# Gate columns of a decoder layer in an opening stage of their own, by seven products of quarters

## Chip, core and metric

The kernel is one layer of a hybrid decoder and runs on one core of a Trainium2 chip. The metric is the time of one execution on the device in microseconds, as the median of repeated runs. The engines are TensorE (PE, with its weight loads PEld), VectorE (DVE), ScalarE (ACT), GpSimd (POOL) and SyncE (SP, whose queue issues most loads; ScalarE's own queue, ACTq, issues most stores).

## Reference, cut to what matters

All tensors are float32: 1024 tokens, model width 1024.

```
z = x @ w_in                        # 1024 x 6152 columns: u | x_lru | g_lru | q | k | v | fg | gate_logits (3 x 1024)
y_s5  = s5(u)                       # diagonal state space, gelu, weight GLU             -> 512
y_lru = gelu(g_lru) * rglru(x_lru)  # conv4, two gates, linear scan over the tokens      -> 512
y_fox = attention(q, k, v, cumsum(log_sigmoid(fg + b_f)))  # 8 heads x 64, causal, 128-query blocks -> 512
proj  = [y_s5, y_lru, y_fox] @ w_branch                    # three products 512 -> 1024
gates = sigmoid(gate_logits + b_gate)                      # one gate per branch and column
mixed = (gates * proj).sum(over branches) @ w_out
x = LN(ALPHA * x + mixed)
x = LN(ALPHA * x + (silu(x @ w_gate) * (x @ w_up)) @ w_down)   # hidden 2816
```

The gate logits are half of the columns of the first product, and only the sum of the three gated projections reads them.

## The kernel before, in words

**Arithmetic.** Each operand of a matmul is split into a rounded high part (ScalarE copies it to fp32r) and a low rest (DVE subtracts), in `split` (L142); `mm3` (L119) makes three matmuls of 128x128 by 128x512 of each product: high by high, high by low, low by high.

**Columns.** `load_x` (L179) loads 128 tokens, PE transposes them (L190) and the parts go to the tiles `x` and `m`. `zblock` (L200) makes 128 columns of z for all tokens: `wcols` (L170) loads 512 KB of weights into a staging tile `ws` (three buffers) and splits it into `wh` and `wl` (two buffers each), and `zpart` (L194) makes each half of the tokens from 8 x 3 = 24 matmuls into a PSUM tile `b` (three buffers) and hands it to a sink. The sink of a gate block (L487) takes tanh (L490) and stores the result to DRAM (`gate_d`).

**Three streams.** `fox` (L381) makes V, Q and K of a pair of heads, after those of pair 0 the forget sums, then `attention` (L360) goes through 8 heads in turn. A step of it is 128 queries: scores on PE into the single score tile `s` (L113, two PSUM banks, one buffer), a masked reduce with the head's bias row on DVE (L320 for the diagonal block with `ndk`, L323 for the columns left of it with `nck`), exp on ScalarE (L324), a scale; after two steps transposes and the value products follow. The bias row of a head comes by a broadcast load (L302) of `ck_d`, and GpSimd masks it (L303); `nck` and `ndk` have one buffer each. `others` makes the columns of u, x_lru and g_lru, then the 24 gate blocks, then the merges of branches 0 (S5) and 1 (RG-LRU): `merge` (L515) multiplies a branch by `w_branch` and by the gates that it loads again. `side` makes the S5 branch in four quarters, its GLU, and then the recurrence, whose four blocks each end with tanh, reciprocal (L848), sqrt (L850), scan (L854), a store (L857) and, for merge 1, a reload and split (`reload`, L499).

**Order.** A loop at the end takes the next step from the stream with the least accumulated cost; each `yield` adds an assumed cost, T_Z = 15 after a column block, T_AT0 and T_AT1 for an attention step. That is the program order; a scheduler with a model of the engines then sets the order of each engine's own instructions, within the data's dependences. Behind the streams come merge 2, the output product, a layer norm, and the feed-forward stage from about 1005 us on, which already works by seven products: its 22 blocks of gate and up columns use sums of quarters, with weight sums by GpSimd and evictions by DVE.

Of the kernel before, what the change touches and what calls it, by code (L numbers as in the profile page):

```python
# [13 lines left out]
F32 = mybir.dt.float32  # L14
# [23 lines left out]
T_AT0 = 1.2  # L38
T_AT1 = 0.473
T_FOX = 10.0  # L40
T_Z = 15.0
T_M = 6.16
T_S5 = 1.44
T_LRU = 1.246
# [13 lines left out]
def trunk(ctx: ExitStack, tc: tile.TileContext, A: dict, out: bass.AP):  # L58
# [12 lines left out]
    pools["side"] = side_stack.enter_context(tc.tile_pool(name="side", bufs=1, side="left"))  # L71
    pools["fox"] = fox_stack.enter_context(tc.tile_pool(name="fox", bufs=1, side="right"))


    SLOTS = {
        "x": ("sb", 8), "m": ("sb", 8), "ws": ("sb", 3), "wh": ("sb", 2), "wl": ("sb", 2),
        "s": ("side", 9), "q": ("fox", 8), "pt": ("fox", 4), "tr": ("fox", 2), "nck": ("fox", 1), "ndk": ("fox", 1),
    }

    LATE = {  # L80
        "ws": ("keep", 4), "w": ("keep", 8), "x": ("keep", 9), "m8": ("mid", 4), "ln": ("mid", 2),
# [5 lines left out]
    def name(n):  # L87
        count[0] += 1
        return f"{n}{count[0]}"

    def new(tag, dt=F32, shape=(P, 1024)):
        pool, bufs = SLOTS[tag]
        return pools[pool].tile(list(shape), dt, name=name(tag), tag=tag, bufs=bufs)

    def half_tile(dt=F32):
        return pools["sb"].tile([P, 512], dt, name=name("zs"), tag="zs", bufs=3)

    def small(shape, dt=F32, name_="c"):
        return const.tile(list(shape), dt, name=name(name_))
# [28 lines left out]
    def tt(e, o, a, b, op):  # L128
        return pin(e.tensor_tensor(o, a, b, op))  # L129
# [16 lines left out]

    ident = small([P, P], name_="ident")
    make_identity(nc, ident)
    tri = scr_([P, P])
    POOL.memset(tri, 1.0)  # L150
    POOL.affine_select(tri, tri, pattern=[[1, P]], compare_op=ALU.is_ge, fill=0.0, base=0, channel_multiplier=-1)
    ones = scr_([P, P])
    POOL.memset(ones, 1.0)
# [22 lines left out]

    x_in, w_in = A["x"], A["w_in"]

    def load_x(tb):  # L179
        h, c = tb // 4, slice((tb % 4) * P, (tb % 4 + 1) * P)  # L180
        xt = new("s")
        SP.dma_start(xt, x_in[tb * P : (tb + 1) * P, :])
        for kp in range(4):
            if tb % 4 == 0:
                XH[h][kp] = new("x", F32R, (P, 2, 512))
                XL[h][kp] = new("m", F32R, (P, 2, 512))
            pa = bank([P, 2, P], "ab"[kp % 2])
# [61 lines left out]

    NF = NT * HEADS  # L250
# [130 lines left out]
    def fox():  # L381
        order = [0, 1, 2, 3]
        for p in order:
# [58 lines left out]
    first_k = done["k"]  # L442


    rows = few("nat", [124, P], 1, "side")

    def put_rows(r, ap, c=slice(0, P)):
        SP.dma_start(rows[r : r + ap.shape[0], c], ap)

    put_rows(0, A["b_gate"].rearrange("(n p) -> n p", p=P))  # L450
    put_rows(24, A["lru_conv_w"].rearrange("k (n p) -> (k n) p", p=P))
    put_rows(40, A["lru_conv_b"].rearrange("(n p) -> n p", p=P))
    put_rows(44, A["lru_b_a"].rearrange("(n a) d -> n (a d)", a=2))
    put_rows(48, A["lru_b_x"].rearrange("(n a) d -> n (a d)", a=2))
    put_rows(52, A["lru_lambda"].rearrange("(n p) -> n p", p=P))
    put_rows(56, A["s5_b_glu"].rearrange("(n p) -> n p", p=P))
    for c in (slice(0, 64), slice(64, P)):
        put_rows(60, A["s5_a_re"], c)
        put_rows(92, A["s5_a_im"], c)
    pr = bank()  # L460
    PE.transpose(pr[:, 0:124], rows, ident[0:124, 0:124])
    cols = small([P, 124], name_="cols")
    DVE.tensor_copy(cols, pr[:, 0:124])
    half = small([P, 60], name_="half")
    ts(DVE, half, cols[:, 0:60], 0.5, ALU.mult)
# [5 lines left out]
    gate_d = dram.tile([3, NK, P, S], F32, name="gate_d")  # L471

    def plain_sink(dst):
        def sink(h, ps):
# [5 lines left out]
    def u_sink(b):  # L480
        def sink(h, ps):
            st = half_tile()
            ACT.copy(st.rearrange("p (j c) -> p c j", j=8), ps.rearrange("p (c j) -> p c j", j=8))
            ACT.dma_start(u_d[b][:, :, 64 * h : 64 * h + 64], st.rearrange("p (j c) -> p j c", j=8))
        return sink

    def gate_sink(r):  # L487
        def sink(h, ps):
            st = half_tile()
            ACT.activation(st, ps, AF.Tanh, bias=half[:, r : r + 1], scale=0.5)  # L490
            ACT.dma_start(gate_d[r // NK, r % NK][:, 512 * h : 512 * h + 512], st)
        return sink


# [853 lines left out]
```

## Time and profile before

| | |
|---|---|
| median of 3 runs | 1660.53 us (1660.35 to 1661.82) |
| profiled execution, its span | 1665.8 us, 1664.1 us |
| PE busy | 1600.4 us, 96% of the span |
| PEld | 1326.4 us, 80% |
| DVE | 1010.8 us, 61% |
| ACT | 633.9 us, 38% |
| POOL | 600.7 us, 36% |
| PE's share of the chain that ended last | 77% (DVE 8%, DMA 5%) |
| mean granted TensorE clock | 0.984 |

The span runs from the first to the last instruction of the profiled execution. Busy time counts an engine's instructions without its waits. The chain that ended last is followed back from the last instruction to whatever released each step. Shares of the whole span mix stages; the rows further below are by stage.

### The profile page before, as it was taken

The page shows a single profiled execution, that of the slowest core. Times are in us where ns is not written, and L with a number is a line of the kernel's source. Part 1 is how long each engine was busy: PE and PEld are TensorE (multiplying, and loading weights), DVE is VectorE, ACT ScalarE, POOL GpSimd, SP SyncE. Part 2 cuts the span into 40 slices and gives each one's busy share as a digit, 9 for nine tenths or more (in the row PEclk, how much of TensorE's full clock was granted, in tenths as well). Part 3 has the DMA queues.
Part 4 walks back from the last instruction along what each step waited for, and adds up shares of the span by engine and source line. Part 5 has one row for each costly group of instructions (what it writes and reads, how often), then busy time and mean ns, then how long its engine had stood idle before and what let it go on. Part 6 is the DMA issues. An engine that isn't in the chain of part 4 may idle for free.

```text
span 1664.1 us, 20521 instructions
## 1 busy us (share of the span) xinstructions
PE 1600.4 (96%) x7482; PEld 1326.4 (80%) x7482; DVE 1010.8 (61%) x1602; ACT 633.9 (38%) x960; POOL 600.7 (36%) x529
## 2 busy tenths in 40 slices
PE   8989998999989999999999998999999999999997
PEld 6877887877877888888888886888888888778886
DVE  4746575633643366967758659675555555546766
ACT  4324454433543354656213224222222222244442
POOL 0111314442234011111140017599988788500004
PEclk9999999999989999999999998999999999999999
DMA  5332233333233334335654812356544445597752
GB/s 167 75 89 72 70 91 89 93 73 95 84 74 89 97 108 143 104 120 196 220 175 155 274 51 80 123 178 202 180 162 165 165 155 175 200 336 234 243 176 101
DMA packets 219968, 236.09 MB, mean 142 GB/s; under 512 B 33376, under 2 KB 162524, under 8 KB 219868
## 3 DMA queue, kind: packets, MB, share of 16 engines
q1 hardware_dynamic: 192604, 202.83, 39.1%
q10 hardware_dynamic: 27264, 31.96, 5.9%
q8 instruction: 59, 0.97, 0.2%
q14 instruction: 41, 0.34, 0.1%
HBM read 163.96 MB, written 70.78 MB: 141 GB/s over the span
## 4 chain that ended last, share of the span: by engine, by line
PE 77%; DVE 8%; DMA 5%; issue 4%; POOL 3%; ACT 2%; SPq 1%; ACTq 0%; DVEq 0%; POOLq 0%
PE p L117 34%; PE b L117 33%; PE a L117 8%; DMA nck<-ck_d 2%; PE s L117 2%; POOL s L129 1%; PE a L341 1%; DMA ws<-w_ffn_down 1%; DVE r L129 1%; DVE s L129 1%; POOL ln L129 1%; DVE wl L129 1%; DVE m L129 1%; ACT r L1235 1%; DMA row<-ln_b 1%
## 5 line engine op out<-in xcount | busy, mean ns | idle before, releaser
L117 PE MATMUL b<-x,wh 128*128 128x512 f32 x912 | 353.6, 399 | 2.3 <-ACT s L706 1.7
L117 PE MATMUL b<-x,wl 128*128 128x512 f32 x832 | 330.0, 397 | 0.0
L117 PE MATMUL b<-m,wh 128*128 128x512 f32 x784 | 310.8, 396 | 0.0
L117 PE MATMUL p<-mx,w 128*128 128x512 f32 x1056 | 250.5, 392 | 1.8 <-DVE mx L129 1.0
L117 PEld LDWEIGHTS p<-mx,w 128*128 128x128 f32 x1056 | 200.0, 190 | 44.3 <-POOL m L129 1.4
L117 PEld LDWEIGHTS b<-x,wh 128*128 128x128 f32 x912 | 173.9, 191 | 37.1 <-ACT s L706 2.0
L117 PEld LDWEIGHTS b<-x,wl 128*128 128x128 f32 x832 | 158.3, 190 | 32.4
L129 DVE TENSOR_TENSOR x<-x,p 128x512 f32<-128x512 f32 x163 | 108.4, 683 | 109.6 <-PE p L117 92.7
L117 PEld LDWEIGHTS b<-m,wh 128*128 128x128 f32 x784 | 149.9, 191 | 29.1 <-issue 0.2
L117 PE MATMUL p<-w,w 128*128 128x512 f32 x528 | 157.5, 390 | 1.2 <-DVE w L129 1.0
L129 POOL TENSOR_TENSOR s<-s,s 128x1024 f32<-128x1024 f32 (+9 forms) x76 | 77.5, 1020 | 207.4 <-ACT s L850 73.8
L129 DVE TENSOR_TENSOR w<-ws,w 128x1024 fp32r<-128x1024 f32 x88 | 115.3, 1316 | 52.7 <-ACT w L143 52.5
L143 ACT CAST w<-ws 128x1024 fp32r<-128x1024 f32 x88 | 92.1, 1050 | 110.5 <-PE p L117 72.6
L117 PE MATMUL p<-wo,w 128*128 128x512 f32 x528 | 127.3, 389 | 0.0
L129 DVE TENSOR_TENSOR wl<-ws,wh 128x1024 fp32r<-128x1024 f32 x62 | 85.3, 1376 | 65.7 <-ACT wh L143 62.4
L117 PEld LDWEIGHTS p<-w,w 128*128 128x128 f32 x528 | 98.8, 188 | 23.3 <-DVE w L129 2.9
L117 PEld LDWEIGHTS p<-wo,w 128*128 128x128 f32 x528 | 99.1, 188 | 20.6
L143 ACT CAST wh<-ws 128x1024 fp32r<-128x1024 f32 x62 | 65.1, 1050 | 125.1 <-PE b L117 94.4
L129 DVE TENSOR_TENSOR w<-m,w 128x1024 fp32r<-128x1024 f32 x44 | 67.6, 1536 | 63.5 <-ACT w L143 63.5
L129 POOL TENSOR_TENSOR ln<-x,x 128x512 f32<-128x512 f32 x44 | 75.7, 1726 | 64.0 <-ACT x L1170 52.6
L117 PE MATMUL p<-w 128*128 128x512 f32 x264 | 97.5, 390 | 1.1 <-ACT w L143 1.1
L129 POOL TENSOR_TENSOR r<-r,row 128x1024 f32<-128x1024 f32 x7 | 16.7, 2389 | 189.9 <-DVE r L129 184.7
(276 smaller groups left out, 2730.0 us busy)
## 6 DMA issues: line engine op xcount, KB each, us to landing
ws<-w_in SPq DMA_DIRECT2D x48, 512.0 KB, 4.5
ws<-w_ffn_gate SPq DMA_DIRECT2D x27, 512.0 KB, 4.5
gate_d<-zs ACTq DMA_DIRECT2D x48, 256.0 KB, 2.0
zs<-gate_d SPq DMA_DIRECT2D x48, 256.0 KB, 2.6
ws<-w_ffn_up SPq DMA_DIRECT2D x22, 512.0 KB, 4.7
x<-w_ffn_down SPq DMA_DIRECT2D x22, 512.0 KB, 5.5
hid_d<-ln SPq DMA_DIRECT2D x22, 512.0 KB, 4.2
wts_d<-x SPq DMA_DIRECT2D x22, 512.0 KB, 2.6
```

What stands on the lines that cost most here:

```text
L117: PE.matmul(o, a, b, start=first, stop=last)
L129: return pin(e.tensor_tensor(o, a, b, op))
L143: pin(ACT.copy(hi, src))
L341: PE.transpose(ta[:, j, e, :], pts[e][:, (k0 + j) * P : (k0 + j + 1) * P], ident)
L1235: pin(ACT.activation(r, r, AF.Identity, bias=nm, scale=rs))
```

## The change

A stage ahead of everything else makes all 24 gate blocks, two at a time (12 pairs of neighbouring blocks), and stores their tanh to `gate_d` as before. For a pair the tokens are cut into two halves, the inner dimension into two halves and the two blocks are the two halves of the columns, so that the product is one of 2x2 by 2x2 quarters; it is made by seven products of sums of quarters, each 4 x 3 = 12 matmuls of 128x512, where the plain form has eight such products. The sums of x (`s1` to `s4`, split into high and low) are made once, in `load_x`, when the second half of the tokens comes in; the sums of weights are four adds per pair on GpSimd; the quarters of the result are added on DVE, and tanh reads them from SBUF. The stage has memory pools of its own, which are closed behind it. V of pair 0 becomes a plain `zblock`, the gate loop leaves `others`, the small parameter rows are loaded by ACTq, and T_Z goes from 15 to 40.

```diff
-T_Z = 15.0
+T_Z = 40.0
...
+    EARLY = {
+        "x": ("sb", 8), "m": ("sb", 8), "ws": ("early", 3), "w": ("early", 8), "t": ("early", 9), "m8": ("early", 1),
+    }
...
     def load_x(tb):
...
+            if h == 0:
+                tt(POOL, rawx[j][:, e], hi.bitcast(F32), lo.bitcast(F32), ALU.add)
+            elif kp < 2:
+                tt(DVE, s3[:, e], s3[:, e], pa, ALU.subtract)
+            else:
+                e = slice(2 * kp - 4, 2 * kp - 2)
+                tt(POOL, x22[:, e], hi.bitcast(F32), lo.bitcast(F32), ALU.add)
+                tt(DVE, s1[:, e], pas[kp - 2], x22[:, e], ALU.add)
+        if h == 0:
+            return
+        tt(POOL, s2, x22, s3, ALU.subtract)
+        tt(POOL, s4, s4, s2, ALU.subtract)
+        for n, src, e in (("s2", s2, POOL), ("s3", s3, DVE), ("s1", s1, DVE), ("s4", s4, POOL)):
...
+            ACT.copy(hi, src)
+            tt(e, lo, src, hi.bitcast(F32), ALU.subtract)
...
+    EP = [(b, d) for b in range(3) for d in range(0, NK, 2)]
...
+    EPRE = 4
...
+    def early_sums(p):
+        ER[p] = [early_cols(p, e) for e in range(2)]
...
+        tt(POOL, t1, w12, w11, ALU.subtract)
+        tt(POOL, t2, w22, t1, ALU.subtract)
+        tt(POOL, t3, w22, w12, ALU.subtract)
+        tt(POOL, t4, w21, t2, ALU.subtract)
...
+    def xop(i, k):
+        if i in (1, 2, 4):
+            h, k = {1: (0, k), 2: (0, 4 + k), 4: (1, 4 + k)}[i]
+            return xh(h, k), xl(h, k)
+        return [t[:, k] for t in SX[{3: "s4", 5: "s1", 6: "s2", 7: "s3"}[i]]]
...
+    def early_product(i, p):
+        ps = bank(tag="ba"[turns[0] % 2])
+        turns[0] += 1
+        for k in range(4):
+            mm3(ps, EW[p][i][0][:, k], EW[p][i][1][:, k], *xop(i, k), k == 0, k == 3)
+        return ps
...
+    load_x(0)
+    early_parts(0, early_cols(0, 0), 1, 2)
+    for tb in range(1, 4):
+        load_x(tb)
+    early_parts(1, early_cols(1, 0), 1, 2)
...
+    for p in range(EPRE):
+        early_begin(p)
+        early_first(p)
+        if p < 2:
+            load_x(4 + 2 * p)
+            load_x(5 + 2 * p)
+            early_parts(2 + p, early_cols(2 + p, 0), 1, 2)
+        if p == 2:
+            early_sums(0)
+            early_b(0)
+        if p == 3:
+            early_c(0)
+    pinned[0] = True
+    early_sums(1)
+    early_middle(0)
+    for p in range(len(EP)):
...
+        p5 = early_product(5, p)
...
+        tt(DVE, s1, u2, early_product(7, p), ALU.add)
+        tt(DVE, u3, s1, p5, ALU.add)
+        tt(DVE, u2, u2, p5, ALU.add)
+        early_gate(p, 1, 1, u3)
...
+        tt(DVE, s1, s1, early_product(4, p), ALU.add)
+        early_gate(p, 0, 1, s1)
+        tt(DVE, u2, u2, early_product(3, p), ALU.add)
+        early_gate(p, 1, 0, u2)
+    pinned[0] = False
...
             if p == order[0]:
-                load_x(0)
-                w = wcols(w_in, C_V + p * P)
-                for tb in range(1, NT):
-                    load_x(tb)
-                for h in range(2):
-                    zpart(w, h, v_sink)
+                zblock(C_V + p * P, v_sink)
...
-        for b in (0, 1, 2):
-            for d in range(NK):
-                zblock(C_G + b * D + d * P, gate_sink(b * NK + d))
-                yield T_Z
```

`early_begin` makes product 1 of a pair, `early_first` product 2 and with it the first quarter of the result, `early_middle` product 6. `early_parts`, `early_b` and `early_c` split the weight quarters and their sums. While `pinned` is set, copies and adds of the stage keep the order of the program.

**SyncE's queue at the start.** Before, the eight x blocks (`s`, 128x1024) follow each other, with one weight block (`ws`) among them:

```order
L182 DMA s_102<-x 128x1024
L172 DMA ws_132<-w_in 128x8x128
L182 DMA s_138<-x 128x1024
L182 DMA s_160<-x 128x1024
L182 DMA s_182<-x 128x1024
L182 DMA s_204<-x 128x1024
L182 DMA s_234<-x 128x1024
L182 DMA s_256<-x 128x1024
L182 DMA s_278<-x 128x1024
L172 DMA ws_368<-w_in 128x8x128
```

In the changed kernel the x blocks are the tiles `t`:

```order
L189 DMA t_88<-x 128x1024
L294 DMA ws_123<-w_in 128x8x128
L294 DMA ws_210<-w_in 128x8x128
L294 DMA ws_361<-w_in 128x8x128
L189 DMA t_129<-x 128x1024
L294 DMA ws_478<-w_in 128x8x128
L294 DMA ws_515<-w_in 128x8x128
L294 DMA ws_517<-w_in 128x8x128
L189 DMA t_156<-x 128x1024
L294 DMA ws_566<-w_in 128x8x128
L189 DMA t_183<-x 128x1024
```

Seven weight blocks have moved ahead of the fourth x block.

**TensorE in the first head.** Before, the scores (`s` from `q`, `q`) and value products (`a` from `tr`, `q`) of a step stand between column matmuls (`b` from `x` or `m` and a weight):

```order
L117 MATMUL b_1740<-x_227,wh_1702 128x512
L117 MATMUL a_999<-tr_1001,q_100 128x256
L117 MATMUL b_1740<-m_228,wh_1702 128x512
L117 MATMUL s_985<-q_96,q_94 128x512
L117 MATMUL s_985<-q_98,q_94 128x512
L117 MATMUL s_985<-q_96,q_94 128x256
L117 MATMUL s_985<-q_98,q_94 128x256
L117 MATMUL a_999<-tr_1001,q_100 128x256 x3
```

In the changed kernel, at the second to fourth step of the same head (transposes of the exponentials are `a` from `ident`, `pt`):

```order
L122 MATMUL s_2561<-q_2017,q_2015 128x256
L122 MATMUL s_2561<-q_2019,q_2015 128x256
L529 MATMUL a_2600<-ident_77,pt_2548 128x128
L122 MATMUL s_2574<-q_2017,q_2015 128x384
L122 MATMUL s_2574<-q_2019,q_2015 128x384
L529 MATMUL a_2600<-ident_77,pt_2560 128x128 x2
L122 MATMUL s_2587<-q_2017,q_2015 128x512
L122 MATMUL s_2587<-q_2019,q_2015 128x512
L122 MATMUL a_2599<-tr_2601,q_2021 128x256
L529 MATMUL a_2710<-ident_77,pt_2573 128x128
```

The column matmuls have left this place; three scores stand with only three transposes among them.

**TensorE behind the last block of the recurrence.** Before, the last gate matmuls of the recurrence (`b` from `s`, `s`) are followed by merge 0 (`a` from `x`, the reloaded S5 branch):

```order
L117 MATMUL b_6966<-s_6945,s_6121 128x512
L117 MATMUL b_6966<-s_6946,s_6121 128x512
L117 MATMUL b_6966<-s_6945,s_6122 128x512
L117 MATMUL a_7031<-x_6978,wl_7003 128x512
L117 MATMUL a_7031<-x_6984,wh_7002 128x512
L117 MATMUL a_7031<-x_6985,wh_7002 128x512
L117 MATMUL a_7031<-x_6984,wl_7003 128x512
```

In the changed kernel they are followed by merge 1 (`b` and `a` from `s_7520`, the first reloaded block of the recurrence's result):

```order
L122 MATMUL b_7500<-s_7479,s_6777 128x512
L122 MATMUL b_7500<-s_7480,s_6777 128x512
L122 MATMUL b_7500<-s_7479,s_6778 128x512
L122 MATMUL b_7556<-s_7520,wh_7544 128x512
L122 MATMUL b_7556<-s_7521,wh_7544 128x512
L122 MATMUL a_7573<-s_7520,wh_7544 128x512
L122 MATMUL a_7573<-s_7521,wh_7544 128x512
```

Merge 0 has moved ahead of the recurrence's last block, and nothing else stands between that block and the product that reads its result.

## Rows read from the trace of the kernel before

**Rows 1.** Stages: stretch, its length, busy us (count) per engine, granted clock, DMA.

```profile
core 0: us, PE busy (x) PEld busy (x) DVE busy (x) ACT busy (x) POOL busy (x), PEclk, DMA share, GB/s
120.00:706.00 586.00, 556.72 (x2844) 467.82 (x2845) 326.00 (x684) 270.25 (x488) 160.12 (x237) 0.97 0.34 91
706.00:826.00 120.00, 119.23 (x547) 98.70 (x546) 88.25 (x77) 56.64 (x69) 15.55 (x6) 1.00 0.52 175
1045.00:1425.00 380.00, 378.95 (x1672) 313.50 (x1671) 217.29 (x227) 103.80 (x138) 310.18 (x199) 1.00 0.51 170
```

**Rows 2.** The same view, 40 us of the feed-forward stage.

```profile
1080.00:1120.00 40.00, 40.00 (x178) 33.12 (x177) 29.24 (x29) 11.51 (x15) 37.41 (x24) 1.00 0.52 172
```

**Rows 3.** Grouped lines, ScalarE, 0 to 880 us: busy, mean ns, idle before.

```profile
L143 ACT CAST wh<-ws 128x1024 fp32r<-128x1024 f32 x60 | 63.0, 1050 | 125.1 <-PE b L117 94.4 <-PE a L117 24.8 <-DVE ho L129 3.9
L490 ACT ACTIVATE zs<-b,half 128x512 f32<-128x512 f32 x48 | 33.0, 687 | 49.8 <-PE b L117 48.9 <-issue 0.4
```

**Rows 4.** Timeline, start of the span, TensorE: start, duration, instruction, wait before.

```profile
4.85 0.66 PE L190 MATMUL a<-ident,s 128*128 128x128 f32 x2 [4.85 <-DMA s<-x]
17.83 0.50 PE L117 MATMUL b<-x,wh 128*128 128x512 f32 x1 [0.22 <-DVE m L129]
```

**Rows 5.** Grouped lines, GpSimd, whole span.

```profile
L129 POOL TENSOR_TENSOR m<-ws,m 128x512 f32<-128x512 f32 x44 | 70.6, 1605 | 1.6
L129 POOL TENSOR_TENSOR x<-x,x 128x512 f32<-128x512 f32 x28 | 40.4, 1443 | 17.5 <-ACT x L992 12.5 <-DVE x L129 3.2
L129 POOL TENSOR_TENSOR mx<-x,mx 128x512 fp32r<-128x512 f32 x7 | 10.3, 1473 | 108.3 <-ACT mx L973 108.3
L129 POOL TENSOR_TENSOR s<-s,s 128x256 f32<-128x256 f32 x8 | 6.1, 766 | 0.0
```

**Rows 6.** One tile's instructions: ns min/median/max, first and last start, forms.

```profile
L320 DVE CUSTOM_DVE_ANT_0 pt<-s,ndk x64: 216/292/306, 119.8 to 706.0; 128x128 f32<-128x128 f32 x64
L117 PE MATMUL s<-q,q x192: 220/389/735, 53.4 to 704.4; 128*128 128x512 f32 x96, 128*128 128x128 f32 x32, 128*128 128x256 f32 x32, 128*128 128x384 f32 x32
```

**Rows 7.** Grouped lines, VectorE, 0 to 880 us.

```profile
L129 DVE TENSOR_TENSOR wl<-ws,wh 128x1024 fp32r<-128x1024 f32 x60 | 82.9, 1381 | 65.7 <-ACT wh L143 62.4 <-PE b L117 2.7
L323 DVE CUSTOM_DVE_ANT_0 pt<-s,nck,st 128x896 f32<-128x896 f32 x8 | 9.2, 1145 | 0.2
```

**Rows 8.** Timeline, TensorE, 425 to 490 us: value products and small products.

```profile
448.30 0.64 PE L117 MATMUL a<-tr,q 128*128 128x256 f32 x4
449.69 2.48 PE L117 MATMUL b<-s,s 128*128 128x128 f32 x20
```

**Rows 9.** The bias row's tile: mask on GpSimd, and its load from issue to landing.

```profile
L303 POOL TENSOR_SCALAR_AFFINE_SELECT ndk<-nck x8: 1091/1091/1092, 118.7 to 648.4; 128x1024 f32<-128x1024 f32 x8
...
DMA to landing us min/median/max: 9.0/9.1/10.1
```

**Rows 10.** Timeline, change from head 0 to head 1.

```profile
149.66 0.22 DVE L320 CUSTOM_DVE_ANT_0 pt<-s,ndk 128x128 f32<-128x128 f32 x1
...
152.29 0.38 SPq L302 DMA_DIRECT2D nck<-ck_d  x1
...
161.79 0.29 DVE L320 CUSTOM_DVE_ANT_0 pt<-s,ndk 128x128 f32<-128x128 f32 x1 [7.12 <-POOL ndk L303]
```

**Rows 11.** Timeline, last block of the recurrence and first of merge 1.

```profile
782.45 1.52 PE L117 MATMUL b<-s,s 128*128 128x512 f32 x6
...
814.91 1.23 DVE L129 TENSOR_TENSOR s<-ws,s 128x1024 fp32r<-128x1024 f32 x1 [3.43 <-ACT s L143]
...
826.42 0.61 PE L117 MATMUL b<-s,wh 128*128 128x512 f32 x2
```

**Rows 12.** Stages of 5 us, end of the first layer norm.

```profile
1005.00:1010.00 5.00, 1.17 (x6) 0.63 (x4) 5.00 (x4) 2.22 (x5) 5.00 (x4) 1.00 0.00 0
1010.00:1015.00 5.00, 2.17 (x8) 1.43 (x8) 4.96 (x7) 0.15 (x1) 5.00 (x4) 0.62 0.13 52
1015.00:1020.00 5.00, 4.52 (x11) 3.56 (x12) 5.00 (x6) 2.71 (x5) 3.71 (x3) 0.50 0.13 53
```

More of the change, by code (lines that the diff above doesn't have):

```diff
@@ L70, in trunk @@
     pools = {"sb": sb, "const": const}
[L71 to L76, printed above, removed]
+    early_stack = ExitStack()
+    pools["early"] = early_stack.enter_context(tc.tile_pool(name="early", bufs=1, side="left"))
+    pools["sums"] = early_stack.enter_context(tc.tile_pool(name="sums", bufs=1, side="right"))
+    EARLY = {
+        "x": ("sb", 8), "m": ("sb", 8), "ws": ("early", 3), "w": ("early", 8), "t": ("early", 9), "m8": ("early", 1),
+    }
+    MIXERS = {
+        "x": ("sb", 8), "m": ("sb", 8), "ws": ("work", 3), "wh": ("work", 2), "wl": ("work", 2),
         "s": ("side", 9), "q": ("fox", 8), "pt": ("fox", 4), "tr": ("fox", 2), "nck": ("fox", 1), "ndk": ("fox", 1),
     }
+    SLOTS = dict(EARLY)
     LATE = {
@@ L95, in half_tile @@
     def half_tile(dt=F32):
-        return pools["sb"].tile([P, 512], dt, name=name("zs"), tag="zs", bufs=3)
+        return pools["work"].tile([P, 512], dt, name=name("zs"), tag="zs", bufs=3)
     def small(shape, dt=F32, name_="c"):
@@ L148, in trunk @@
     make_identity(nc, ident)
[L149 to L153, printed above, removed]
     eps_t = small([P, 16], name_="eps")[:, 0:1]
@@ L247, in softplus_neg, with early_cols, early_parts @@
         return p
+    gate_d = dram.tile([3, NK, P, S], F32, name="gate_d")
+    EP = [(b, d) for b in range(3) for d in range(0, NK, 2)]
+    EW = [dict() for _ in EP]
+    EG = [None] * len(EP)
+    ER = {}
+    EPRE = 4
+    def early_cols(p, e):
+        b, d = EP[p]
+        c0 = C_G + b * D + (d + e) * P
+        t = new("ws", shape=(P, NK, P))
+        SP.dma_start(t, w_in[:, c0 : c0 + P].rearrange("(k p) c -> p k c", p=P))
+        return t
+    def early_parts(p, src, i, j):
+        hi, lo = [new("w", F32R, (P, NK, P)) for _ in range(2)]
+        split(src, hi, lo)
+        EW[p][i], EW[p][j] = [[t[:, c] for t in (hi, lo)] for c in (slice(0, 4), slice(4, 8))]
@@ new lines, in early_sums, with early_b @@
+    def early_sums(p):
+        ER[p] = [early_cols(p, e) for e in range(2)]
+        w11, w21, w12, w22 = [ER[p][e][:, c] for e in range(2) for c in (slice(0, 4), slice(4, 8))]
+        t = new("m8", shape=(P, 16, P))
+        t1, t2, t3, t4 = [t[:, 4 * i : 4 * i + 4] for i in range(4)]
+        tt(POOL, t1, w12, w11, ALU.subtract)
+        tt(POOL, t2, w22, t1, ALU.subtract)
+        tt(POOL, t3, w22, w12, ALU.subtract)
+        tt(POOL, t4, w21, t2, ALU.subtract)
+        ER[p].append(t)
+    def early_b(p):
+        early_parts(p, ER[p][2][:, 0:8], 5, 6)
+        v = new("t", F32R, (P, NK, P))
+        split(ER[p][1][:, 4:8], v[:, 0:4], v[:, 4:8])
+        EW[p][3] = [v[:, 0:4], v[:, 4:8]]
@@ new lines, in early_gate, with early_begin, early_first @@
+    def early_gate(p, e, h, y):
+        b, d = EP[p]
+        r = b * NK + d + e
+        pin(ACT.activation(y, y, AF.Tanh, bias=half[:, r : r + 1], scale=0.5))
+        ACT.dma_start(gate_d[b, d + e][:, 512 * h : 512 * h + 512], y)
+    def early_begin(p):
+        t = new("t", shape=(P, 2, 512))
+        EG[p] = [t[:, 0], t[:, 1]]
+        pin(ACT.copy(EG[p][0], early_product(1, p)))
+    def early_first(p):
+        s1, y = EG[p][:2]
+        tt(DVE, y, s1, early_product(2, p), ALU.add)
+        early_gate(p, 0, 0, y)
@@ new lines, in early_middle, with put_rows @@
+    def early_middle(p):
+        t = new("t", shape=(P, 2, 512))
+        EG[p] += [t[:, 0], t[:, 1]]
+        tt(DVE, t[:, 0], EG[p][0], early_product(6, p), ALU.add)
+    load_x(0)
[3 more added lines that the diff above has]
+    early_parts(1, early_cols(1, 0), 1, 2)
+    rows = few("nat", [124, P], 1, "early")
+    def put_rows(r, ap, c=slice(0, P)):
+        ACT.dma_start(rows[r : r + ap.shape[0], c], ap)
+    put_rows(0, A["b_gate"].rearrange("(n p) -> n p", p=P))
@@ new lines, in trunk @@
+    pr = bank(tag="a")
+    PE.transpose(pr[:, 0:124], rows, ident[0:124, 0:124])
+    cols = small([P, 124], name_="cols")
+    DVE.tensor_copy(cols, pr[:, 0:124])
+    half = small([P, 60], name_="half")
+    ts(DVE, half, cols[:, 0:60], 0.5, ALU.mult)
+    for p in range(EPRE):
[10 more added lines that the diff above has]
+            early_c(0)
@@ L250, in trunk @@
+    pinned[0] = False
+    early_stack.close()
+    SLOTS.clear()
+    SLOTS.update(MIXERS)
+    pools["work"] = sb_stack.enter_context(tc.tile_pool(name="work", bufs=1, side="left", reuse_waits="tile"))
+    pools["side"] = side_stack.enter_context(tc.tile_pool(name="side", bufs=1, side="left", reuse_waits="tile"))
+    pools["fox"] = fox_stack.enter_context(tc.tile_pool(name="fox", bufs=1, side="right", reuse_waits="tile"))
     NF = NT * HEADS
@@ L442, in trunk @@
     first_k = done["k"]
[L445 to L465, printed above, removed]
     u_d = dram.tile([NB, P, 8, P], F32, name="u_d")
```

59 lines of the change are left out of this document (47 added, 12 removed).

## Prediction

> **What bounds the kernel now.** I read the busy times stage by stage first, then the grouped lines of each engine, then the order of the two programs beside the trace's timeline. TensorE (PE) is busy 1600.4 of 1664.1 us, and the stages show that it bounds nearly all of them: from the first attention step to the last (120 to 706 us) PE is busy 556.7 of 586 us while VectorE (DVE) is busy 326.0, from 706 to 826 us PE is busy 119.2 of 120, and in the feed-forward stage it never stops [rows 1]. So PE time saved is time saved, as long as PE stays the engine that the others wait for. A 128x512 matmul in a full stream costs 40 us / 178 = 0.2247 us [rows 2].
>
> The gate columns are 24 blocks; their 48 halves appear as 48 tanh evictions on ScalarE [rows 3]. Each half is 24 matmuls, so 1152 matmuls, 258.9 us of PE. They need nothing but x and weights and nobody waits for them until the merges. The order puts them between the attention steps: they are the work that PE does while DVE handles a softmax. That is the second thing the change touches.
>
> **The arithmetic.** Seven quarter products of 12 matmuls for 12 pairs are 1008 matmuls, 226.5 us. Against 258.9 that is 144 matmuls fewer, 32.4 us. Everything below is what this gain meets.
>
> **The start of the new stage.** Before, the first x block reaches PE at 4.85 us and the first column matmul runs at 17.83 us, with all eight x blocks transposed [rows 4]. After, SyncE's queue has three weight blocks ahead of x block 1, three more ahead of block 2 and one ahead of block 3, and from the fourth on a weight load waits for a staging buffer that a split must free. With the trace's first landing, and a split of 1.05 us on ScalarE plus 1.38 us on DVE behind each landing [rows 3, 7], I put block 2 at about 17, block 3 at about 21 and the first product at about 24 us. Products 1 and 2 of four pairs (96 matmuls, 21.6 us) need only the first half of x. Product 6 needs s2, a sum over the second half that GpSimd makes from block 4 on, after the first pair of products (about 32 us). Per block GpSimd does two adds of 128x256 at 0.766 us, two of 128x512 at 1.443 and two splits of 128x512 at 1.473: 7.4 us, 29.5 for four, plus one set of weight sums that stands between (four adds, 1.6 us each, 6.3 us), less the last split, which product 6 doesn't need: 32 + 29.5 + 6.3 - 1.5 = 66 us [rows 5]; I take 67. Bounds: 58, if GpSimd is as fast as its best rows and never waits, and 75, if transposes wait for PSUM buffers that GpSimd holds up.
>
> From there 912 matmuls remain, 205 us at the stream's rate. Per pair DVE has four splits and seven evictions (about 10 us), GpSimd 6.4 us, PE 18.9 us; the feed-forward stage has the same mix with PE full [rows 1, 2]. The stage ends at 67 + 205 = 272 us. Before, the gate columns and the 17.8 us ahead of them cost 276.7. So of 32.4 us about 28 go in the start, and the stage gives 5.
>
> **The first attention step.** V, Q and K of pair 0 take 144 matmuls, 32.4 us, plus 1.5 for the first weight split: K ends at 306. Before, the first score stands right behind K at 53.4 us and the first reduce comes at 119.8 [rows 6]: 66 us in which DVE builds the forget sums and S5 parameters and the bias row is stored and reloaded. Between K and the second score stand 255 matmuls of 512 columns before, with small ones 58 us of PE, and 200 after, 48 us. I take 63 us for the chain (48 if PE's work covered it): first reduce at 369 us.
>
> **The attention steps.** One PSUM tile of two banks holds every score (its pool has one buffer), so score k+1 waits for the reduces of step k: PE and DVE meet 64 times. I cut the order of each engine at these 64 places and added the trace's row durations (reduces 0.29 to 1.15 us [rows 6, 7], a value matmul of 256 columns and a small one of 128 each 0.12 us [rows 8]). From the second score to the last, before: PE 518, DVE 351 (7% above the busy time in rows 1, since short instructions overlap), and the sum over the steps of the busiest engine 550 us; the trace took 585 [rows 6]. PE led in 43 of 62 steps. After: PE 333, DVE 332, sum of the busiest 434; PE leads in only 23 steps. Column and merge matmuls between the two scores are 936 instead of 1754, and the later steps of head 0 have none. The trace shows the excess of 35 us at the head changes: the bias row is loaded once the last reduce is done, and the load takes 9.1 us to land, then GpSimd masks it in 1.09 us, so a head change takes 12 us even where little is to be done [rows 9, 10]. After, four of seven changes have 6.0, 6.0, 7.8 and 7.2 us of work in that step: 12.4 less these is 22.6 us; two at a change of pairs keep the 7 to 9 us that they have before, one has enough DVE work: 38 us together. So 369 + 1 + 434 + 38 = 842 us for the last reduce.
>
> The Trainium skill (DMA: Bandwidth & Descriptors, Anatomy of one DMA) prices a DMA at about 2.0 us plus its bytes over 436 GB/s; for this 512 KB row its estimate would be 3.2 us, head changes would nearly vanish, and the sum would be some 38 us lower. The trace's 9.1 us differs and decides here.
>
> **Behind attention.** Before, 958.1 us pass from the last reduce to the end. The order has 63.3 us less PE work there (859.5 for 922.8). But the last recurrence block loses its cover. Its matmuls end at 783.97 us; tanh, reciprocal, scan, a store, a reload and a split follow, ready at 816.14: 32.2 us, and PE enters merge 1 only at 826.42, busy with gates and merge 0 all the while [rows 11]. After, its last matmul is followed at once by merge 1, of which 12 matmuls (2.7 us) can run: 29 us of PE idle. Bounds 20 (ScalarE and the queues less crowded) and 32. Ahead of it DVE has 60 us of work for PE's 57, which I price at 3. So 842 + 958.1 - 63.3 + 32 = 1769 us of span.
>
> The profiled execution has 1665.8 us for a span of 1664.1, and the median of the runs is 1660.53: +1.7 - 5.3. **Forecast 1766 us, 6.4% slower.** By differences: -32.4 (arithmetic), +28 (start), +8 (first step), +72 (attention: 139 us over PE's work instead of 67), +32 (recurrence), about +107 with rounding.
>
> **Rivals.**
> 1. *Queues run ahead and fill the steps.* If PE and DVE overlap over a whole head rather than a step, the busiest engine by head sums to 378 instead of 434; with the start at 58, the first step's chain at 48, the head changes at 23 and the tail at 22 the span is 263 + 34 + 48 + 1 + 378 + 23 + 958 - 63 + 22 = 1664, the median about 1660: no change or a little faster. For it: before, PE is nearly full. Against it: the single score tile, and before's 585 us lie above the sum by step, not below. It takes every low end at once; with half of them it is 1700 to 1720. 9%.
> 2. *Half clock.* From 1005 to 1015 us PE worked only 3.3 of 10 us, and the granted clock fell to 0.62 and then 0.50, which is 1.2 GHz, and was still there while PE worked 4.5 of the next 5 us [rows 12]. In the 39 steps that PE doesn't lead it has 113 us of work; at half speed 44 us of it stick out over the other engines: 1810. The Trainium skill (TensorE: Matmul & The Clock Gate, What's actually happening) says that the throttled clock is the default and activity lifts it, which speaks against a stage with half-idle PE. 15%.
> 3. *The early loop isn't PE's.* Its single buffer for weight sums and three staging buffers make a ring: split, sums, split, about 15 us of a pair's 18.9. At 22 us a pair 12 pairs add 37 us: 1803. The feed-forward stage speaks against it, with more buffers. 8%.
> 4. *The start is hidden* (58 instead of 67) with the rest as forecast: 1757, inside my range.
>
> **How the numbers follow.** The forecast has 65% with its own range of 1715 to 1805. The range of 1695 to 1820 takes in half of rival 1's ends and both slow rivals and leaves out about 2 in 10. A measurement here tells 0.2% (3.3 us) from no change. Faster: two thirds of rival 1, 6%; same: 3%; slower: 91%.
>
> **What would show it.** Product 6 waiting for GpSimd at 60 to 70 us; PE full from there to about 270; first reduce near 369; in attention PE waiting for reduces (L320 and L323 of before) in long total, a PE share near 70% and several stretches of low clock; head changes of 12 us; one PE gap near 29 us ahead of merge 1; the feed-forward stages unchanged. If PE is still over 90% busy from the first reduce to the last, the step argument is wrong; if the first product 6 runs before 50 us, the start is.

## Result: 1797.5 us for 1661.2, and the profile after

The changed kernel takes 1797.47 us (median of 4 runs, 1795.4 to 1799.05), the kernel before 1661.17 beside it (1660.35 to 1663.83). The ratio is 1.0817, 95% interval 1.0798 to 1.0836: slower by 136 us, where 105 were forecast. The time lies inside the stated range, at its upper part.

The page of the profiled execution after, its head:

```profile
span 1796.8 us, 20639 instructions
PE 1613.0 (90%) x7338; PEld 1327.2 (74%) x7338; DVE 1099.9 (61%) x1734; ACT 672.6 (37%) x1012; POOL 708.3 (39%) x614
...
PE   5799997879789879886776999899999999999997
...
PEclk9899998979999889997797999899999999999999
```

There are 144 matmuls less, and TensorE is busy 12.6 us longer. Busy time times one less the granted clock, summed over the span, is 51 us for 18 before: in TensorE's busy time the low clock alone takes back the 32.4 us of arithmetic. The other 12 us are not traced to a place; matmuls that stand alone, without overlap, are the likely one. Its idle time grew from 63.7 to 183.8 us. Where that lies, the stages of the changed kernel show (columns as in [rows 1]):

```profile
core 0: us, PE busy (x) PEld busy (x) DVE busy (x) ACT busy (x) POOL busy (x), PEclk, DMA share, GB/s
0.00:70.00 70.00, 40.58 (x163) 32.19 (x164) 38.65 (x68) 31.89 (x63) 53.45 (x58) 0.88 0.48 143
70.00:276.00 206.00, 206.00 (x910) 170.65 (x910) 94.35 (x121) 72.27 (x94) 51.82 (x41) 1.00 0.33 103
276.00:286.00 10.00, 1.24 (x4) 0.70 (x4) 1.29 (x2) 1.76 (x2) 0.00 (x0) 0.66 0.65 181
286.00:330.00 44.00, 42.61 (x183) 34.15 (x182) 15.81 (x32) 14.20 (x21) 0.96 (x1) 0.96 0.27 61
330.00:390.00 60.00, 45.62 (x204) 35.77 (x203) 43.31 (x175) 14.74 (x19) 18.30 (x16) 0.93 0.36 73
390.00:861.00 471.00, 396.82 (x2005) 328.31 (x2006) 296.86 (x665) 235.93 (x438) 158.55 (x234) 0.91 0.31 82
861.00:957.00 96.00, 62.39 (x273) 51.26 (x272) 77.67 (x67) 37.75 (x46) 15.86 (x6) 0.82 0.33 111
1175.00:1555.00 380.00, 378.30 (x1669) 313.07 (x1668) 220.42 (x228) 103.74 (x137) 312.35 (x200) 1.00 0.51 170
```

The first line is the start of the stage, with TensorE idle 29 of 70 us; the second its full part, with no idle time; then the hole between the stage and V, then V, Q and K, the first step's chain, attention (74 us idle at a clock of 0.91, where [rows 1] have 29 us and 0.97), the recurrence's tail (34 us idle), and the feed-forward stage, which is as it was.

The stage's first product and its first product 6 (`sx` are the sums of x), on TensorE:

```profile
23.82 0.78 PE L122 MATMUL b<-x,w 128*128 128x512 f32 x1
...
69.69 2.52 PE L122 MATMUL b<-sx,w 128*128 128x512 f32 x10
```

The hole behind it, on all engines: the stage's last gate store, V's weight load, its split, and V's first matmul.

```profile
278.17 0.33 ACTq L341 DMA_DIRECT2D gate_d<-t  x1
280.26 1.98 SPq L172 DMA_DIRECT2D ws<-w_in  x3
...
284.32 1.04 ACT L148 CAST wh<-ws 128x1024 fp32r<-128x1024 f32 x1 [6.18 <-DMA ws<-w_in]
...
285.42 0.80 PE L122 MATMUL b<-x,wh 128*128 128x512 f32 x1 [8.76 <-ACT wh L148]
```

In attention the reduce and the mask answer to [rows 6] and [rows 9]. The last two lines are the time that VectorE sat idle ahead of the 64 diagonal reduces, and how often, by what ended it: the mask or the score.

```profile
L508 DVE CUSTOM_DVE_ANT_0 pt<-s,ndk x64: 261/291/294, 389.6 to 861.4; 128x128 f32<-128x128 f32 x64
L491 POOL TENSOR_SCALAR_AFFINE_SELECT ndk<-nck x8: 1093/1093/1094, 388.5 to 809.4; 128x1024 f32<-128x1024 f32 x8
...
  POOL ndk L491: 38.4, 5
  PE s L122: 30.9, 16
```

The tail ahead of merge 1 answers to [rows 11]; first VectorE's part of the recurrence's last block, then TensorE:

```profile
933.09 6.54 DVE L996 RECIPROCAL s<-s 128x1024 f32<-128x1024 f32 x1
...
944.63 2.29 DVE L1002 TENSOR_TENSOR_SCAN s<-s,s 128x1024 f32<-128x1024 f32 x1
...
955.42 1.22 DVE L134 TENSOR_TENSOR s<-ws,s 128x1024 fp32r<-128x1024 f32 x1 [6.11 <-ACT s L148]
```

```profile
927.72 2.43 PE L122 MATMUL b<-s,s 128*128 128x512 f32 x10
956.85 1.22 PE L122 MATMUL b<-s,wh 128*128 128x512 f32 x2 [26.70 <-ACT wh L148]
```

TensorE has nothing between the recurrence's last matmuls and merge 1, and its first two matmuls of merge 1 take 1.22 us where [rows 11] have 0.61.

A table that the rest uses, from the traces (us): the first reduce, from there to the last reduce, and from there to the end.

| kernel | first reduce | attention | behind it | span |
|---|---|---|---|---|
| before | 119.8 | 586.2 | 958.1 | 1664.1 |
| changed | 389.6 | 471.8 | 935.4 | 1796.8 |
| b_nogates | 117.5 | 473.0 | 976.8 | 1567.3 |
| b_front | 382.0 | 493.8 | 939.1 | 1814.9 |
| a_h8 | 303.8 | 507.3 | 945.3 | 1756.4 |
| a_h4 | 231.4 | 550.9 | 964.2 | 1746.5 |

In one line: the gate columns now cost 269.8 us ahead of the first reduce, and their absence gives back 137.1 behind it (114.4 in attention, 22.7 later). The difference is the 132.7 us of the spans.

### The profile page after: what moved, and what is told of

Its sections match the earlier page's. It is cut to its first block, busy times and chain, and to the rows that moved or that the text cites. A ratio compares the mean times of both kernels' runs of the same rounds, so it can differ in the third digit from the quotient of the medians.

```text
span 1796.8 us, 20639 instructions
## 1 busy us (share of the span) xinstructions
PE 1613.0 (90%) x7338; PEld 1327.2 (74%) x7338; DVE 1099.9 (61%) x1734; ACT 672.6 (37%) x1012; POOL 708.3 (39%) x614
## 4 chain that ended last, share of the span: by engine, by line
PE 51%; DVE 10%; DMA 5%; ACT 3%; issue 2%; POOL 2%; SPq 0%; ACTq 0%; DVEq 0%; POOLq 0%
PE p L122 31%; PE b L122 12%; PE a L122 6%; DMA nck<-ck_d 2%; DVE s L134 1%; DMA ws<-w_ffn_down 1%; DVE s L142 1%; DVE r L134 1%; DVE pt L511 1%; PE s L122 1%; PE a L529 1%; DVE pt L138 1%; POOL ln L134 1%; DVE x L142 1%; POOL s L134 1%
## 5 line engine op out<-in xcount | busy, mean ns | idle before, releaser
L122 PE MATMUL b<-x,wh 128*128 128x512 f32 x528 | 202.7, 404 | 19.1 <-ACT wh L148 8.8
L122 PE MATMUL b<-x,wl 128*128 128x512 f32 x448 | 179.3, 400 | 0.0
L122 PE MATMUL b<-m,wh 128*128 128x512 f32 x400 | 159.9, 400 | 0.0
L134 DVE TENSOR_TENSOR w<-m,w 128x1024 fp32r<-128x1024 f32 x68 | 97.7, 1436 | 85.5 <-ACT w L148 85.4
L122 PEld LDWEIGHTS b<-x,wh 128*128 128x128 f32 x528 | 101.5, 192 | 41.8 <-ACT wh L148 9.2
L134 POOL TENSOR_TENSOR m<-ws,m 128x512 f32<-128x512 f32 x68 | 100.7, 1481 | 2.5
L134 POOL TENSOR_TENSOR m<-ws,ws 128x512 f32<-128x512 f32 x34 | 50.6, 1488 | 125.6 <-DVE w L134 108.0
L122 PEld LDWEIGHTS b<-x,wl 128*128 128x128 f32 x448 | 86.3, 193 | 18.6 <-DVE wl L134 0.8
L122 PE MATMUL a<-tr,q 128*128 128x256 f32 (+1 forms) x320 | 72.8, 322 | 24.7 <-DVE tr L134 16.8
L148 ACT CAST w<-m 128x1024 fp32r<-128x1024 f32 x68 | 71.1, 1046 | 63.4 <-PE p L122 45.5
```

The source lines that it names most:

```text
L122: PE.matmul(o, a, b, start=first, stop=last)
L148: pin(ACT.copy(hi, src))
```

## Experiments

Ratios are to the kernel before, run on the same chip at the same time.

**b_nogates: the gate columns left out of the kernel before.**

```diff
-        for b in (0, 1, 2):
-            for d in range(NK):
-                zblock(C_G + b * D + d * P, gate_sink(b * NK + d))
-                yield T_Z
+        zblock(C_G, gate_sink(0))
+        yield T_Z
...
-                SP.dma_start(g, gate_d[n, d][:, hs])
+                SP.dma_start(g, gate_d[0, 0][:, hs])
```

> The kernel before with 23 of its 24 gate blocks left out (the merges read the first block's gates in their place), so 1104 matmuls or 248 us of TensorE work less, all of it from between the attention steps. Theory 'cover': the mixers take what their steps' dependences take; the changed kernel, whose mixers have no gate columns either, spends 1796.8 - (330.1 - 53.4) = 1520 us of span outside its early stage, so about 1518 us here, 140 below the kernel before, and two thirds as much TensorE idle time in attention as in the changed kernel or more. Rival 'TensorE bounds': the time falls by the matmuls' own 248 us to about 1413.

Measured: 1568.12 us, ratio 0.9425 (0.9407 to 0.9443). Without 248 us of TensorE's work the kernel is 94 us shorter. That is far from the rival's 1413; it is also 50 us longer than my 1518. Attention is as forecast, 473.0 us beside 471.8 in the changed kernel:

```profile
118.00:590.00 472.00, 403.33 (x2021) 332.74 (x2022) 288.10 (x657) 221.24 (x427) 155.86 (x235) 0.90 0.29 78
590.00:727.00 137.00, 64.61 (x268) 51.24 (x267) 96.17 (x78) 50.06 (x59) 20.53 (x8) 0.72 0.27 92
```

The excess is behind it (976.8 us for 935.4), where with the column step at 15 three waits of the recurrence stand bare on TensorE:

```profile
663.78 1.65 PE L117 MATMUL b<-s,s 128*128 128x512 f32 x3 [15.14 <-ACT s L143]
...
690.86 1.65 PE L117 MATMUL b<-s,s 128*128 128x512 f32 x3 [19.72 <-ACT s L143]
...
726.84 1.22 PE L117 MATMUL b<-s,wh 128*128 128x512 f32 x2 [28.54 <-ACT wh L143]
```

So the gate columns were nearly two thirds hidden in the kernel before.

**b_front: the move alone, with eight products.** The loop over the gate blocks and the rows that it needs stand ahead of V; `T_Z = 40.0`:

```diff
+    load_x(0)
+    w = wcols(w_in, C_G)
+    for tb in range(1, NT):
+        load_x(tb)
...
+    for h in range(2):
+        zpart(w, h, gate_sink(0))
+    for r in range(1, 24):
+        zblock(C_G + r * P, gate_sink(r))
```

> The kernel before with its 24 gate blocks, still eight products, moved whole ahead of V, Q and K of pair 0 (no sums, no seven products; the column step 40 as in the changed kernel). Theory 'cover': the move alone makes it slow. The blocks end at 17.8 + 1152 x 0.2247 = 277 us, about where the early stage of the changed kernel ends, V follows without a wait, and the rest is as in the changed kernel: about 1780 us. Rival 'the stage itself' (its sums, its start, its ring of buffers are what costs): the move alone costs little, 1660 to 1700 us.

Measured: 1813.74 us, ratio 1.0905 (1.0883 to 1.0928). The move, with the column step that goes with it, costs 151 us; the rival, that the stage's sums and start do it, falls. It is also 34 us above my 1780, 22 of them in attention. Its first score comes at 322.6 us, TensorE being full until there, and that of the changed kernel at 330.3: up to this point the seven products give nothing, they lose 8 us, which is no more than the hole of 8.8 that b_front doesn't have. The 16 us by which the changed kernel is nevertheless faster are in attention, 471.8 for 493.8. The mixers' work is the same in both; in b_front's order VectorE does 20 us more of the side work ahead of the last reduce (317.4 us busy for 296.9), and nothing of it comes back behind it (939.1 for 935.4):

```profile
382.00:876.00 494.00, 412.56 (x2047) 339.87 (x2047) 317.40 (x675) 242.81 (x447) 165.83 (x236) 0.89 0.30 82
```

An order alone is thus worth some 20 us here, which has to be kept in mind for small differences below.

**a_ws: staging buffers in the pool that stays open.**

```diff
-        "x": ("sb", 8), "m": ("sb", 8), "ws": ("early", 3), "w": ("early", 8), "t": ("early", 9), "m8": ("early", 1),
+        "x": ("sb", 8), "m": ("sb", 8), "ws": ("sb", 3), "w": ("early", 8), "t": ("early", 9), "m8": ("early", 1),
```

(and the same for `ws` of the mixers.) 

> The changed kernel, with the weights' staging buffers kept in the pool that stays open, so that V's weight load need not wait for memory of the early stage. Theory: of the 9.0 us in which TensorE waits between the early stage and V (276.4 to 285.4 us) 7 to 9 go, 1788 us. Rival: the load waits for its place in SyncE's queue or for its buffers anyhow: within 2 us of 1797.

Measured: 1817.46 us, ratio 1.0928 (1.0906 to 1.0949). V's weights are now loaded at 249.5 us in place of 280.3, but the split's target still lies in memory of the early stage and waits for the last gate store. ScalarE's and TensorE's first work on V:

```profile
282.43 1.99 ACT L148 CAST wh<-ws 128x1024 fp32r<-128x1024 f32 x2 [3.08 <-DMA gate_d<-t]
283.52 0.79 PE L122 MATMUL b<-x,wh 128*128 128x512 f32 x1 [5.66 <-ACT wh L148]
```

The hole shrinks from 8.8 to 5.7 us. So the staging buffers' memory caused 3 us of it; that the rest waits for the last stores is what the trace names, and no run took it away. As a whole the kernel is 20 us slower, outside both ranges, since attention takes 492.6 us, as in b_front; of the hole's price at the end the run tells nothing.

**a_m0: merge 0 held back.**

```diff
+        while "lru3" not in done:
+            yield 5.0
         for b in range(NB):
             fetch(0, b)
...
+            if b == NB - 1:
+                done["lru3"] = True
```

> The changed kernel, with merge 0 held back until the last block of the recurrence is begun. Theory 'the tail lost its cover': the gap of 26.7 us ahead of merge 1 closes for the most part, 1770 to 1787 us. Rival: the recurrence is a chain that needs its time anyway, and merge 0 only leaves a gap of 20 us or more where it stood before (890 to 930 us): within 4 us of 1797.

Measured: 1800.18 us, ratio 1.0829 (1.0812 to 1.0846): the rival is right on the time, though the gap that comes back is 15 us and not 20. TensorE's longest wait between the last reduce and merge 1, and the start of merge 1:

```profile
920.66 1.65 PE L122 MATMUL b<-s,s 128*128 128x512 f32 x3 [15.33 <-ACT s L148]
...
964.17 0.73 PE L122 MATMUL b<-s,wh 128*128 128x512 f32 x2 [0.96 <-ACT wh L148]
```

The gap ahead of merge 1 is gone and merge 1 starts 98 us after the last reduce, as before (95). Covering the recurrence's last block uncovers the one before: TensorE idles 31 us from the last reduce to merge 1, for 34 in the changed kernel. The gap is where the length of the recurrence's chain shows, not its cause.

**a_side7: the recurrence earlier.** `T_S5` and `T_LRU` times 0.7, `T_Z` 20.

> The changed kernel with the assumed costs of the steps of S5 and recurrence times 0.7 and the column step 20 in place of 40, so that the order has the whole recurrence ahead of the last attention steps. Theory: of the 95 us from the last reduce to merge 1, in which TensorE idles 34 us, the recurrence's chain goes beside attention, whose engines all have idle time: 15 to 30 us less, 1767 to 1782 us, with the tail gap gone. Rival: attention grows by what the tail loses, since VectorE works in both: within 5 us of 1797.

Measured: 1806.97 us, ratio 1.0870 (1.0854 to 1.0887). Attention and tail, two windows:

```profile
388.00:957.00 569.00, 468.94 (x2231) 380.60 (x2230) 367.79 (x717) 272.05 (x478) 179.27 (x243) 0.88 0.31 86
957.00:1050.00 93.00, 90.29 (x411) 74.75 (x410) 65.89 (x91) 28.19 (x40) 23.27 (x16) 0.98 0.50 161
```

Behind attention the end comes 847.7 us after the last reduce (935.4 in the changed kernel), and attention grows from 471.8 to 569.2. What the tail loses attention pays, and 10 us more; the time is outside both ranges, on the rival's side.

**a_nck2: two buffers for the bias row**, the next head's row asked for at step 4 of each head.

```diff
-        "s": ("side", 9), "q": ("fox", 8), "pt": ("fox", 4), "tr": ("fox", 2), "nck": ("fox", 1), "ndk": ("fox", 1),
+        "s": ("side", 9), "q": ("fox", 8), "pt": ("fox", 4), "tr": ("fox", 2), "nck": ("fox", 2), "ndk": ("fox", 2),
...
-            bias = head_bias(hd)
+            bias = biases.pop(hd) if hd in biases else head_bias(hd)
...
+                if i0 == 4 and hd + 1 < HEADS:
+                    biases[hd + 1] = head_bias(hd + 1)
```

> The changed kernel with two buffers for the bias row and its mask; a head's row is asked for in the middle of the head before. Theory: the 38.4 us in which VectorE waits for the mask at five head changes are on the path, since nothing covers them in these mixers: 25 to 35 us less, 1762 to 1772 us. Rival: the steps behind a head change are late for other reasons, and the wait only moves: within 5 us of 1797.

Measured: 1790.28 us, ratio 1.0772 (1.0756 to 1.0788): 7 us, not 25 to 35. The mask's tile again:

```profile
  PE s L122: 44.0, 20
  POOL ndk L491: 9.9, 1
```

The waits for the mask fall from 38.4 to 9.9 us, 13 come back as waits for scores, and attention takes 461.6 us, 10 less. From reduce to reduce, the four head changes within a pair now take 3.6, 6.3, 6.9 and 4.4 us, 28 less together than the 10.6, 12.2, 12.3 and 14.3 of the changed kernel; other steps take 18 more. These four changes were not idle: they held 30 us of TensorE's work (at the stream's rate), and much of it now stands in other steps. With an order alone worth some 20 us, 10 is a rough figure.

**b_nck2: the same edit in the kernel before.** 

> The kernel before with two buffers for the bias row and its mask, as in a_nck2. TensorE idles 29 us from the first reduce to the last and owes 11 us more to its clock; VectorE waits 27.3 us for the mask at four head changes. Theory: part of this idle time hangs on the head changes: 6 to 15 us less, 1646 to 1655 us. Rival: the gate columns cover the head changes already: within 3 us of 1661.

Measured: 1651.82 us, ratio 0.9939 (0.9924 to 0.9955): 0.6% faster than the kernel before, which is little but clear of the noise, and inside the theory's range. Attention takes 573.7 us for 586.2, with the work the same as in [rows 1]:

```profile
118.00:691.00 573.00, 553.04 (x2845) 464.73 (x2846) 324.82 (x682) 270.14 (x488) 161.05 (x237) 0.98 0.35 94
```

**a_dummy: four matmuls that nobody reads in each attention step.**

```diff
+                    pz = bank()
+                    for z in range(4):
+                        mm(pz, xh(0, z)[:, 0:P], xh(0, z), z == 0, z == 3)
                     yield T_AT0 + T_AT1 * (i + 1)
```

> The changed kernel with four more matmuls of 128x512 that nobody reads in each of the 64 attention steps (256 in all, 57.5 us of TensorE at the stream's rate). Theory 'clock': TensorE's low clock in attention (30 us of its busy time there is owed to it) is on the path, and the filler lifts it: 10 to 30 us less, 1767 to 1787 us, granted clock above 0.97. Theory 'waits': the path goes through VectorE and the chain of a step, TensorE's low clock lies in its slack, and the filler costs only in the steps that TensorE leads: 0 to 20 us more, 1797 to 1817 us.

Measured: 1819.13 us, ratio 1.0938 (1.0917 to 1.0959).

```profile
385.00:879.00 494.00, 440.33 (x2263) 365.63 (x2264) 305.73 (x670) 241.14 (x445) 166.12 (x238) 0.94 0.30 78
```

The clock in attention rises from 0.91 to 0.94, not above 0.97, and the time rises too, by 22 us for 57.5 us of filler, 2 us over the range of 'waits'. The run can't part the two theories cleanly, since the filler has a price of its own: with the filler in, the sum over the steps of the busier engine (it is explained in the next section) is 451 us for 421, 30 more, so that some 8 us could have come back by the clock or by another order.

**a_half: two steps in one score tile.** Steps 0 and 1, and 2 and 3, write the two halves of one tile.

```diff
+        if i < 4:
+            if i % 2 == 0:
+                shared[0] = wide()
+            ps = shared[0][:, 512 * (i % 2) : 512 * (i % 2) + 512]
+        else:
+            ps = wide()
```

> The changed kernel, with steps 0 and 1, and 2 and 3, of each head in the two halves of one score tile, so that 16 of the 64 scores don't wait for the reduces of the step before. Theory 'lockstep at the score tile': 10 to 25 us less, 1772 to 1787 us. Rival: the wait at the score tile only stands for VectorE's time and the chain behind it: within 5 us of 1797.

Measured: 1797.21 us, ratio 1.0811 (1.0795 to 1.0827). Its first reduce and TensorE's next score:

```profile
389.75 0.29 DVE L515 CUSTOM_DVE_ANT_0 pt<-s,ndk 128x128 f32<-128x128 f32 x1 [10.36 <-POOL ndk L491]
```

```profile
390.10 0.80 PE L122 MATMUL s<-q,q 128*128 128x256 f32 x2 [3.50 <-DVE st L515]
```

The score in the other half still starts at the end of the first reduce: the edit did not take away the wait that it was to take away, and says nothing on either theory. A score tile with two full buffers was not tried.

**a_scaleact: scaling on ScalarE.**

```diff
-        ts(DVE, pt[:, 0:n], pt[:, 0:n], rl, ALU.mult)
+        ACT.activation(pt[:, 0:n], pt[:, 0:n], AF.Copy, scale=rl)
```

> The changed kernel, with the scaling of the exponentials by one over their sum on ScalarE in place of VectorE (64 instructions, some 35 us of VectorE's 296 in attention). Theory 'VectorE leads the steps': 10 to 30 us less, 1767 to 1787 us. Rival 'the chain of a step leads, whichever engine does its links': within 5 us of 1797.

Measured: 1806.58 us, ratio 1.0873 (1.0854 to 1.0892).

```profile
392.00:875.00 483.00, 408.67 (x2051) 338.87 (x2051) 280.30 (x615) 293.56 (x516) 159.82 (x236) 0.90 0.31 84
```

VectorE has 17 us less to do there, since side work fills half of the 35 us, ScalarE 58 us more, and attention is 11 us longer (482.6 us). The time is outside both ranges. That speaks against 'VectorE leads the steps', but for the rival only weakly: over the span the scalings take 49 us on ScalarE for 35 on VectorE, so the link itself became longer, and a difference smaller than what an order is worth could hide in it.

**a_h8 and a_h4: 8 and 16 gate blocks back between the attention steps.**

```diff
-    EP = [(b, d) for b in range(3) for d in range(0, NK, 2)]
+    EP = [(b, d) for b in range(3) for d in range(0, NK, 2)][:8]
...
+        for r in range(16, 24):
+            zblock(C_G + r * P, gate_sink(r))
+            yield T_Z
```

(`[:4]` and `range(8, 24)` in a_h4.) 

> The changed kernel with the 8 gate blocks of the third branch back between the attention steps, by eight products as before (early stage of 8 pairs, column step 24). Four pairs less are 75.6 us less of early stage; 384 matmuls, 86.3 us, come back to the mixers. Theory 'cover': they cost there no more than the 94.5 us that 23 blocks cost in the kernel before over the one without them, 4.1 us a block, and less while there is much idle time: 1722 to 1755 us. Rival 'TensorE bounds the mixers': they cost their own 86 us: 1808 us.

> The same with 16 gate blocks back (early stage of 4 pairs, column step 18): 151 us less of early stage, 16 blocks back at 4.1 us each or a little over: 1700 to 1725 us, still over the kernel before, since the arithmetic saved by 4 pairs is 10.8 us and the start of the stage costs more. If the first blocks come back for nothing and only the last cost their full time, 1690. Rival (TensorE bounds): about 1818.

Measured: 1758.32 us, ratio 1.0582 (1.0557 to 1.0607), and 1748.18 us, ratio 1.0514 (1.0497 to 1.0532). Their attention:

```profile
304.00:811.00 507.00, 458.29 (x2342) 382.07 (x2342) 309.94 (x669) 250.18 (x460) 162.43 (x237) 0.95 0.32 84
```

```profile
231.00:782.00 551.00, 506.77 (x2571) 424.45 (x2571) 298.61 (x668) 253.51 (x467) 160.16 (x237) 0.95 0.33 84
```

Behind the first reduce (attention and the rest together, from the table) the kernels take 1407.2, 1452.6, 1515.1 and 1544.3 us with 0, 8, 16 and 24 blocks there: 5.7 us a block on the average, not the 4.1 that I took from b_nogates, and so both came out above my ranges, a_h4 by 23 us. The price isn't even: 5.7, 7.8 and 3.7 us a block from each kernel to the next, each with its own column step and order. The 10.8 us of TensorE that a block holds were never charged.

## Why the prediction was right, point by point

**Start of the stage: right.** The first product runs at 23.8 us (24 forecast), the first product 6 at 69.7 (67), behind GpSimd's sums; then TensorE is full, and the stage ends at 276.7 (272).

**First attention step: 21 us too small.** The step that failed is "K ends at 306". It allowed 1.5 us between the stage and V. The trace has 8.8: V's weights go into memory of the early stage, whose last reader is the last gate store, issued at 278.2, and the load is issued at 280.3 and split at 284.3. K's matmuls end at 323.2, 17 us late: 5 by the stage, 7 by the hole, and 5 because V, Q and K took 37.8 us for 32.4, with transposes among them and the first matmuls at the low clock. The chain behind K takes 66.4 us (63 forecast, 66.4 before). I named what a moved step issues and what queues it passes, and did not ask which memory it inherits.

**Attention: 471.8 us, 473 forecast, and the parts come out too, if roughly.** The trace can be cut much as the forecast was: at the 64 diagonal reduces, with TensorE's matmuls at the stream's rate (0.2247 us for 512 columns, no less than 0.12) and VectorE's durations added up. That is my estimate from the trace's rows. TensorE then has 352 us (333 forecast) and VectorE 331 (332); TensorE leads in 23 of 63 steps (23 forecast); the busier engine sums to 421 us (434). Of the 51 us above that sum, 41 lie in the seven head changes (38 forecast) and 10 in all other steps (1). So the path was right, by steps and head changes, and that the sum is right to 1 us is luck: 13 too much in the steps met 12 too little elsewhere. What a head change holds is not what a second buffer gives back: a_nck2 takes 19 of the 41 us away, as good as all that the four changes within a pair hold (22.6 forecast), and 9 of these come back in other steps.

The sign "a PE share near 70%" failed: the share is 84%, TensorE being busy 397 us, of which the low clock is 32. By this cut, which counts VectorE's overlapping instructions in full (it is busy 297 us), the chain of a step through three engines can set the pace of no more than those 10 us and the head changes.

The row's load takes 9.6 us here from issue to landing, 9.1 in [rows 9], which the forecast used. An estimate by the Trainium skill (DMA: Bandwidth & Descriptors, Anatomy of one DMA) is 3.2 us, by a price that the section fits to DMAs issued from GpSimd, while SyncE issues this one. The measurement differs again.

**The recurrence's tail: 26.7 us of bare wait, 29 forecast, but its place was no lever.** From the last reduce to merge 1 the changed kernel takes 95.5 us (89 forecast), and a_m0, where it is 98 us with merge 0 held back, and a_side7, where attention pays for it, speak for the recurrence's length and against merge 0's place. Behind attention all is 935.4 us for 926.8.

**Sum.** 20.6 late at the first reduce, 1.2 early in attention, 8.6 late behind: 28 us of span, 1796.8 for 1769.

**Rivals.** *Queues run ahead* (1660) fell: TensorE idles 74 us in attention. *Half clock* (1810) came near in time, but not by its mechanism. In the gap ahead of merge 1, with TensorE idle since 930 us, the clock does fall to 0.50, which is 1.2 GHz, and is still there while TensorE works again:

```profile
940.00:950.00 10.00, 0.00 (x0) 0.00 (x0) 9.25 (x6) 0.00 (x0) 2.91 (x1) 0.50 0.10 40
950.00:960.00 10.00, 3.15 (x8) 2.48 (x9) 3.67 (x3) 3.13 (x3) 0.00 (x0) 0.50 0.70 229
```

In attention, taking busy time times one less the clock over stretches of 5 us, TensorE owes about 30 us to it (11 before). But by the cut above the steps outside the head changes take only 10 us more than the busier engine at full clock, where the rival had 44 in all; how much of the head changes' 41 us is the clock stays open, and a_dummy bounds a gain only at some 8 us. *The early loop isn't TensorE's* (1803) came nearest in time, 6 us off, and fell: 206 of 206 us busy. *The start is hidden* (1757) fell: product 6 at 69.7 us, not 58.

**What stays open.** How much of attention's 472 us is the single score tile; how much of it is the order, as the changed kernel with the column step of 15 was not run by itself; and the last 8 us of the tail.

## What to carry to other kernels

Work that TensorE does while another engine handles a chain is paid at its price on the path, not at its busy time: here some 4 to 8 us for a block of 10.8. Taken out and done by itself it costs its full time, and an eighth less arithmetic does not make up for that. Ask of any such move what the work was hiding, what memory the next stage inherits from the new one, and test the price by leaving the work out.

## What the runs showed of the hardware

The attention steps took 472 to 475 us in the changed kernel, a_m0 and b_nogates and 493 to 494 in a_ws and b_front, with the same steps in another order. By the cut at the reduces the difference lies in the steps' own work (442 and 445 us for 421) and not in the waits (51 and 49 for 51). It is as much as many an edit here is worth. Behind the gap ahead of merge 1 the granted clock was still 0.50, and two matmuls that take 0.61 us at full clock in [rows 11] took 1.22. The load that broadcasts one row takes 9.6 us, where the other DMAs of 512 KB that the page of the changed kernel lists have medians of 2.6 to 5.8; why, no run shows.
